# A Macaron block on one core: the first three down products made inside the last feature tile, loads written in program order, and split rooms that don't overlap

## The chip, the cores and the metric

The kernel runs on one core of a Trainium2 chip. Its time is the device time of one execution in microseconds (us); the kernel before takes 871.24 us (median of three runs, 870.94 to 872.25).

## The reference

One layer over 512 tokens of width 1,024, all in float32:

```python
x = x + 0.5 * swiglu_ffn(rmsnorm(x, g1), w_gate1, w_up1, w_down1)   # feature width 2816
x = x + hybrid_mixer(rmsnorm(x, gm), ...)                           # attention heads and trailing-mean pooling
x = x + 0.5 * swiglu_ffn(rmsnorm(x, g2), w_gate2, w_up2, w_down2)
x = rmsnorm(x, g3)

def swiglu_ffn(x, w_gate, w_up, w_down):
    return (silu(x @ w_gate) * (x @ w_up)) @ w_down
```

The change touches the two feed-forward stages. Tolerances are those of float32, so the kernel splits every operand of a matmul into a rounded high part and a low part (`fp32r`) and adds three products: high x high, high x low, low x high (`mm3`, L180).

## The kernel before

**Stages.** First feed-forward stage (0 to about 342 us), mixer (to about 530), second feed-forward stage (to the end). Each feed-forward stage has an upward part (`ffn_up`, L405), which goes through 22 tiles of 128 features (gate and up columns), and a downward part (class `Down`, L625).

**Upward part.** Tiles 0 to 4 are plain products. From tile 5 (`PLAIN`) on, a tile is one step of a loop (L569 to L612) in which the 2 x 2 blocks of weights and tokens are multiplied by seven products in place of eight (the Strassen-Winograd scheme): A11, S3, S2, A22, S1, A12, S4 in this order, each of 12 matmuls of 256 columns. S3 and A22 share a bank (`up_hi`); A11, S2, S1 share another (`acc`), and so does the last product, S4, which starts it anew after S1 has been copied out (L595, in `copy`, L559). Inside the loop the orders of PE, ACT and DVE are as written (`tc.manual_schedule`); `fetch(n + 2)` loads the raw weights of the tile after the next into one of two rooms of 2,048 columns (`down.pool`, tag `raw`), `sum13`/`sum24` make their block sums in two rooms of 1,024 (`wpool`, tag `raw`), and `high...`/`low...` split them into high parts (ACT) and low parts (DVE). In the last two tiles fetch(22) and fetch(23) find nothing to fetch.

**Downward part.** The 22 feature tiles pair up into 11 rows of blocks, and these into six groups g (five of two, one of one; `groups`, L622). Seven products again, each over the six groups: for each g `product(p6, g, S2, T2)`, `product(p1, g, A11, B11)`, `product(p5, g, S1, T1)`, then S3 x T3, S4 x B22, A12 x B21 and A22 x T4. The first name is a block of activations, the second one of weights. T1 to T4 are sums of weight blocks that GpSimd's DMAs make in DRAM during the upward part (`make_sums`, L671, `wsum`); B11 to B22 are read from `in_wB`. A call of `Down.product` (L744) takes `tokens` (split of the activations: ACT then DVE, and for S2 and A11 an update of the block, L730), `weights` (a load into a raw room, then a split: ACT casts, DVE subtracts), and then the matmuls: 12 of 512 columns per product of a full group. "T2 of pair 0" below is the weights of product T2 for g = 0, and so on; "product n" counts from 1.

**Rooms.** Raw weights go through a ring of rooms (`rooms`, `raw_tile`, L135). After the loop of tiles it is set anew (L619): two of `down.pool`, two of `wpool`, and in the second stage four of the residual pool behind them. Split weights go through a ring of four (`part_tiles`, L146): three rooms in one tile `parts_sb`, high parts from column 0 and low parts from column 3,136 on, 1,024 apart, and a fourth of two tiles of its own (`whi`, `wlo` in the profile). Parts of the loop of tiles start at column 16 (`SHIFT`) of their room and their low part another 32 further; parts of the down products start at column 0.

**Order.** Outside regions of `manual_schedule` the framework's scheduler orders each engine's instructions by program order, readiness and its own estimates, and may put instructions of the down products between those of the loop. The loads of `Down.weights`, of x and of xt go through `load_now` (L175): each alone in a manual region of SyncE (SP). An engine takes its instructions in order, and a DMA that must wait for its room keeps all that is behind it on SP waiting. The residual x is loaded again into its tiles during the first down part (eight loads of 256 KB, after g = 1 in the code); in the second, eight tiles xt and two gain rows (`gb`) are loaded at g = 2. `constants` (L222) loads small constants and, through DRAM, makes the extended bias table `ext_d`.

Of the kernel before, what the change touches and what calls it, by code (L numbers as in the profile page):

```python
# [8 lines left out]
F32 = mybir.dt.float32  # L9
# [7 lines left out]
P = 128  # L17
# [30 lines left out]
def layer(  # L48
# [93 lines left out]
    parts_sb = wpool.tile([P, 2 * (HILO * 1024 + 64)], F32R, tag="parts", name="parts", bufs=1)  # L142
# [3 lines left out]
    def part_tiles(at=0, apart=0):  # L146
# [27 lines left out]

    def load_now(dst, src):  # L175

        with tc.manual_schedule(engines={mybir.EngineType.SP}):
            nc.sync.dma_start(dst, src)
# [43 lines left out]
    def constants():  # L222
# [5 lines left out]

        flat = EXT - REL
        ext = temp()  # L230
        nc.sync.dma_start(ext[:NH, :REL], rel)
        far = temp()
        nc.vector.tensor_copy(far[:NH, :flat], ext[:NH, 0:1].to_broadcast([NH, flat]))
        nc.sync.dma_start(ext_d[:, flat:], ext[:NH, :REL])
        nc.sync.dma_start(ext_d[:, :flat], far[:NH, :flat])
# [169 lines left out]
    def ffn_up(norm, wA, down, loaded):  # L405
# [42 lines left out]
        todo.extend(norm.blocks(down.pool, aside))  # L448

# [117 lines left out]
        with tc.manual_schedule(engines={E.PE, E.DVE, E.Activation}):  # L567
            last_silu = last_place = last_sums = nothing
            for n in range(PLAIN, KF):  # L569
# [32 lines left out]
                nc.vector.tensor_tensor(u[:, :HT], up_lo, u[:, :HT], op=ALU.add)  # L602
                low24(n + 1)
                product(acc, cut(w22, 0, S), S4, False)
# [20 lines left out]
    class Down:  # L625
# [14 lines left out]
        def __init__(self, order, pair, block):  # L640
# [8 lines left out]

            self.steps = sorted(  # L650
# [48 lines left out]

        def weights(self, i, g):  # L700
# [3 lines left out]
            raw = raw_tile()[:, :n]  # L704
# [39 lines left out]
        def product(self, acc, g, a, i, further=False, scale=None):  # L744
# [4 lines left out]
            if self.n_sums < KF:  # L749
                self.make_sums(a[0][:, 0].bitcast(F32))  # L750
# [37 lines left out]
    with tc.tile_pool(name="act1", bufs=1, reuse_waits="tile") as apool:  # L788
# [4 lines left out]
        for g in range(G):  # L793
# [3 lines left out]
            if g == 1:  # L797

                x[:] = residual_tiles()
                for k in range(KD):  # L800
                    load_now(x[k], xT[k])
# [758 lines left out]
```

## Time and profile before

| | |
|---|---|
| median of three runs | 871.24 us (870.94 to 872.25) |
| the profiled execution | 870.76 us, its span 868.6 us |
| mean granted TensorE clock | 0.988 |
| busy: PE, weight loads (PEld), DVE, ACT, POOL | 841.5, 747.5, 710.1, 501.2, 124.3 us |
| DMA | 158.49 MB, 182 GB/s on average |
| tile loop, first stage | about 61 to 223 us |
| down products, first stage | about 231 to 342 us |
| down products, second stage | from 751 us on |

Busy times overlap. PE's matmuls follow each other without a gap where it isn't made to wait, so a window in which PE is busy all of the time and the granted clock is 1.00 is bound by PE. In rows of timelines the first number is the start, the second the duration, and brackets hold the idle time of the engine before the instruction with what ended it.

### The profile page before, as it was taken

What the parts mean: (1) busy time and instruction counts of PE and PEld (TensorE: products, weight loads), DVE (VectorE), ACT (ScalarE), POOL (GpSimd) and SP (SyncE); (2) the same over time, 40 slices, a digit from 0 to 9 for tenths busy, and PEclk for the clock granted to TensorE, in tenths of its full rate; (3) what the DMA queues carried; (4) which work ended last, traced back from release to release, by engine and by line L of the source; (5) the groups of instructions that cost most, each with busy time, mean ns of one, the idle gap of its engine ahead of it and who ended that gap; (6) DMA issues with size and microseconds to landing.
All of it is one profiled execution on the core that took longest, in us unless ns stands there. A gap on an engine that the chain in (4) does not pass through costs nothing.

```text
span 868.6 us, 14124 instructions
## 1 busy us (share of the span) xinstructions
PE 841.5 (97%) x5296; PEld 747.5 (86%) x5296; DVE 710.1 (82%) x1128; ACT 501.2 (58%) x852; POOL 124.3 (14%) x197
## 2 busy tenths in 40 slices
PE   9999999999799999989999999999999999899995
PEld 7889999999688887867877878889999999788885
DVE  7899999999588769686777576969989999777897
ACT  7455565566376546548747556436556556566572
POOL 0113222122300000120020000112222112300011
PEclk9999999999899999999999999999999999999998
DMA  8268979788996663322220136257979788997622
GB/s 290 55 189 222 254 221 242 224 209 196 296 274 199 208 197 114 107 85 86 73 73 25 49 97 231 84 146 211 241 237 236 209 216 213 294 348 248 209 95 97
DMA packets 71955, 158.49 MB, mean 182 GB/s; under 512 B 6080, under 2 KB 29136, under 8 KB 71504
## 3 DMA queue, kind: packets, MB, share of 16 engines
q1 hardware_dynamic: 49088, 111.45, 37.7%
q0 software_dynamic: 22656, 46.14, 24.9%
q8 instruction: 41, 0.67, 0.3%
q14 instruction: 26, 0.21, 0.1%
q10 hardware_dynamic: 144, 0.01, 0.0%
HBM read 153.38 MB, written 50.34 MB: 235 GB/s over the span
## 4 chain that ended last, share of the span: by engine, by line
PE 54%; DVE 4%; ACT 1%; issue 1%; DMA 1%; POOLq 0%; POOL 0%; ACTq 0%
PE mm L183 13%; PE mm L184 13%; PE mm L185 13%; PE a L183 4%; PE a L184 3%; PE a L185 3%; PE a L1175 1%; PE a L1121 1%; DMA raw<-in_wB_dram 1%; PE a L1163 1%; DVE t L1042 1%; PE a L1360 0%; PE a L1050 0%; ACT prob L1102 0%; DVE parts L124 0%
## 5 line engine op out<-in xcount | busy, mean ns | idle before, releaser
L123 ACT CAST parts<-raw 128x1024 fp32r<-128x1024 f32 (+2 forms) x81 | 78.3, 974 | 68.0 <-PE mm L184 19.1
L124 DVE TENSOR_TENSOR parts<-raw,parts 128x1024 fp32r<-128x1024 f32 (+2 forms) x81 | 90.7, 1128 | 21.4 <-ACT parts L123 20.6
L559 ACT ACTIVATE t<-mm 128x256 f32<-128x256 f32 x102 | 39.2, 385 | 109.2 <-PE mm L185 107.0
L680 POOL DMA_DIRECT2D wsum<-in_wB_dram x72 | 71.7, 1148 | 37.5 <-DMA wsum<-wsum 29.7
L183 PE MATMUL mm<-ha,parts 128*128 128x256 f32 x272 | 75.1, 276 | 0.0
L185 PE MATMUL mm<-ha,parts 128*128 128x256 f32 x272 | 75.1, 276 | 0.0
L184 PE MATMUL mm<-ha,parts 128*128 128x256 f32 x272 | 75.1, 276 | 0.0
L678 POOL COPY mark<-t 128x1 f32<-128x1 f32 x40 | 16.2, 404 | 396.8 <-DVE t L592 221.5
L183 PE MATMUL mm<-hhi,parts 128*128 128x512 f32 x160 | 63.3, 399 | 0.2 <-ACT parts L123 0.2
L470 DVE TENSOR_TENSOR parts<-raw,parts 128x512 fp32r<-128x512 f32 x68 | 62.4, 952 | 0.9 <-ACT parts L465 0.8
L185 PE MATMUL mm<-hhi,parts 128*128 128x512 f32 x160 | 62.4, 394 | 0.0
L184 PE MATMUL mm<-hlo,parts 128*128 128x512 f32 x160 | 62.1, 389 | 0.0
L124 DVE TENSOR_TENSOR ah<-acts,ah 128x512 fp32r<-128x512 f32 (+1 forms) x72 | 47.3, 666 | 16.6 <-ACT ah L123 14.4
L465 ACT CAST parts<-raw 128x512 fp32r<-128x512 f32 x68 | 56.4, 830 | 5.0 <-DMA raw<-in_wA_dram 2.5
L123 ACT CAST ah<-acts 128x512 fp32r<-128x512 f32 (+1 forms) x72 | 41.1, 581 | 27.1 <-PE mm L184 20.4
L184 PE MATMUL mm<-parts,ah 128*128 128x512 f32 x136 | 53.1, 391 | 0.0
L183 PE MATMUL mm<-parts,ah 128*128 128x512 f32 x136 | 53.0, 389 | 0.0
L185 PE MATMUL mm<-parts,ah 128*128 128x512 f32 x136 | 52.9, 389 | 0.0
L184 PEld LDWEIGHTS mm<-ha,parts 128*128 128x128 f32 x272 | 51.1, 188 | 0.1
L183 PEld LDWEIGHTS mm<-ha,parts 128*128 128x128 f32 x272 | 51.1, 188 | 0.1
L185 PEld LDWEIGHTS mm<-ha,parts 128*128 128x128 f32 x272 | 51.1, 188 | 0.0
L470 DVE TENSOR_TENSOR wlo<-wsum,whi 128x1024 fp32r<-128x1024 f32 x34 | 41.6, 1225 | 9.7 <-PE mm L185 7.2
(239 smaller groups left out, 2800.6 us busy)
## 6 DMA issues: line engine op xcount, KB each, us to landing
raw<-in_wA_dram SPq DMA_DIRECT2D x87, 512.0 KB, 6.1
wsum<-in_wB_dram POOLq DMA_DIRECT2D x60, 512.0 KB, 7.6
raw<-wsum SPq DMA_DIRECT2D x40, 512.0 KB, 4.6
raw<-in_wB_dram SPq DMA_DIRECT2D x30, 512.0 KB, 4.8
wsum<-wsum POOLq DMA_DIRECT2D x20, 512.0 KB, 5.1
x<-in_xT_dram SPq DMA_DIRECT2D x16, 256.0 KB, 7.3
raw<-in_wQK_dram SPq DMA_DIRECT2D x8, 512.0 KB, 3.5
raw<-in_wO_dram SPq DMA_DIRECT2D x8, 512.0 KB, 3.4
```

The costliest lines, as they stand in the source:

```text
L123: nc.scalar.copy(hi, src)
L124: nc.vector.tensor_tensor(lo, src, hi.bitcast(F32), op=ALU.subtract)
L183: nc.tensor.matmul(acc, a[0], b[0], start=start, stop=False, **more)
L184: nc.tensor.matmul(acc, a[0], b[1], start=False, stop=False, **more)
L185: nc.tensor.matmul(acc, a[1], b[0], start=False, stop=stop, **more)
L465: nc.scalar.copy(hi, src)
L470: nc.vector.tensor_tensor(lo, src, hi.bitcast(F32), op=ALU.subtract)
L559: nc.scalar.activation(dst, src, AF.Copy, scale=scale)
L678: nc.gpsimd.tensor_copy(mark, after[:, 0:1])
L680: nc.gpsimd.dma_start(self.rows(i, g), self.rows(self.terms[i][at], g), **(dict(accum_op=ALU.add) if at else {}),)
L1042: nc.vector.tensor_tensor(q3, q3, rs[:, t, :].unsqueeze(2).to_broadcast([P, 8, HD]), op=ALU.mult)
L1121: nc.tensor.matmul(sc[i][:, :n], qT[pair][0][a][rows, t * P : (t + 1) * P], kT[pair][0][b][rows, :n], start=a + b == 0, stop=a == 1,)
```

## The change

- **Loads.** From tile 2 on up to the end of the first stage, and in the second stage up to the first output, SP's instructions are issued in written order (`in_order`); `load_now` is gone. The loads of the first six weight tiles of the down products (T2, B11, T1 of pairs 0 and 1; `self.ahead`) are written into the last two tiles, in the places of the fetches that find nothing: T2 and B11 of pair 0 together in one room of 2,048 columns, T1 of pair 0 and T2 of pair 1 in the two rooms of the sums, B11 and T1 of pair 1 in the other room of 2,048.
- **First three products.** Their tokens and weights are split at written places inside the last tile (`first_tokens`, `first_weights`); `product` uses them and doesn't make them again.
- **Rings.** The order of the raw rooms after the loop changes (`more`, `own`, `own`, `more`; in the second stage the four rooms of the residual pool ahead of them).
- **Later loads.** x goes one load each behind the loads of products 8 to 15, constants behind 17, the bias table's load, fill and store behind 18, 20 and 25; in the second stage xt behind 8 to 15, the gain rows behind 16 and 17 (`self.then`).
- **Parts' rooms.** Each of the three rooms is 2,112 columns with the high part and the low part inside it, so that no room overlaps the next.

```diff
-    parts_sb = wpool.tile([P, 2 * (HILO * 1024 + 64)], F32R, tag="parts", name="parts", bufs=1)
+    parts_sb = wpool.tile([P, HILO * 2112], F32R, tag="parts", name="parts", bufs=1)
...
-            i = n_own[0] % HILO * 1024
+            i = n_own[0] % HILO * 2112
             n_own[0] += 1
-            hi, lo = (parts_sb[:, i + j * (HILO * 1024 + 64) :] for j in range(2))
+            hi, lo = parts_sb[:, i:], parts_sb[:, i + (1024 if apart else 1088) :]
         return hi[:, at : at + 1024], lo[:, at + apart : at + apart + 1024]
...
         todo.extend(norm.blocks(down.pool, aside))
+        in_order.enter_context(tc.manual_schedule(engines={mybir.EngineType.SP}))
...
                 w11, w13, w24 = (w[n, i][:2] for i in (11, 13, 24))
+                if n == KF - 1:
+                    down.load(new_sum())
+                    down.load(new_sum())
                 product(acc, w11, A11, True)
+                ends = n == KF - 1
...
                 product(up_hi, cut(w13, S, S), S3, True)
-                fetch(n + 2)
+                if n < KF - 2:
+                    fetch(n + 2)
+                else:
+                    down.load(down.pool.tile([P, 4 * S], F32, tag="raw", name=name("raw"), bufs=RAW))
                 high11(n + 1)
                 low11(n + 1)
+                if ends:
+                    down.first_tokens(0)
                 last_sums()
                 sum13(n + 1)
                 copy(z[:, HT:], up_hi, -1.0)
                 product(acc, cut(w24, 0, S), S2, False)
                 copy(u[:, HT:], acc, -1.0)
                 sum24(n + 1)
+                if ends:
+                    down.first_tokens(1)
                 product(up_hi, cut(w24, S, S), A22, False)
                 nc.vector.tensor_tensor(u[:, HT:], up_hi, u[:, HT:], op=ALU.add)
                 down.make_sums(u[:, HT:])
+                if ends:
+                    down.first_weights(0)
                 product(acc, cut(w13, 0, S), S1, False)
                 copy(z[:, :HT], acc)
...
                 high24(n + 1)
+                if ends:
+                    down.first_tokens(2)
                 product(up_lo, cut(w22, S, S), A12, True)
                 nc.scalar.activation(sg[:, HT:], z[:, HT:], AF.Silu)
                 nc.vector.tensor_tensor(u[:, :HT], up_lo, u[:, :HT], op=ALU.add)
                 low24(n + 1)
+                if ends:
+                    down.first_weights(1)
                 product(acc, cut(w22, 0, S), S4, False)
...
             last_silu()
             last_place()
+            down.first_weights(2)
             last_sums()
 
-        rooms[:] = [(down.pool, "raw", RAW, 4 * S)] * RAW + [(wpool, "raw", RAW, 1024)] * RAW
+        own, more = (wpool, "raw", RAW, 1024), (down.pool, "raw", RAW, 4 * S)
+        rooms[:] = [more, own, own, more]
         n_raw[0] = 0
...
+            self.ahead = [(i, g) for g in range(2) for i in (T2, B11, T1)]
+            self.loaded, self.then, self.made = {}, {}, []
...
+        def load(self, room):
+
+            if self.ahead:
+                i, g = self.ahead.pop(0)
+                raw = self.loaded[i, g] = room[:, :1024]
+                src = self.rows(i, g)
+                c = S if tuple(src.shape[1:]) == (groups[g][1], S) else groups[g][1] * P
+                nc.sync.dma_start(raw.rearrange("p (n c) -> p n c", c=c), src)
+                if room.shape[-1] > 1024:
+                    self.load(room[:, 1024:])
+
+        def first_tokens(self, n):
+            self.made.append([self.tokens((S2, A11, S1)[n], 0)])
+
+        def first_weights(self, n):
+            self.made[n].append(self.weights((T2, B11, T1)[n], 0))
+
         def weights(self, i, g):
...
-            raw = raw_tile()[:, :n]
+            raw = self.loaded.get((i, g))
+            new = raw is None
+            if new:
+                raw = raw_tile()[:, :n]
...
         def product(self, acc, g, a, i, further=False, scale=None):
-            a, w = self.tokens(a, g, scale), self.weights(i, g)
+            if self.n_products < len(self.made):
+                a, w = self.made[self.n_products]
+            else:
+                a, w = self.tokens(a, g, scale), self.weights(i, g)
             self.n_products += 1
...
+            for what, *args in self.then.get(self.n_products, ()):
+                what(*args)
             self.mms(acc, g, a, w, further=further)
...
-        ffn_up(n1, wA1, down1, loaded=False)
-        constants()
+        ffn_up(n1, wA1, down1, False, in_order)
+        x[:] = residual_tiles()
+        for k in range(KD):
+            down1.then[8 + k] = [(nc.sync.dma_start, x[k], xT[k])]
+        down1.then[17] = [(constants,)]
+        for k, what in zip((18, 20, 25), extended()):
+            down1.then[k] = [(what,)]
...
-        ffn_up(n3, wA2, down2, loaded=True)
-        xt = [hpool.tile([P, S], F32, tag="h", name=name("xt")) for _ in range(2 * NT)]
-        rooms.extend((xpool, f"x{i}", 1, 2 * S) for i in range(KD // 2))
-        gb = [temp(), temp()]
+        ffn_up(n3, wA2, down2, True, in_order)
+        xt, gb = [None] * (2 * NT), [None] * 2
+        rooms[:0] = [(xpool, f"x{i}", 1, 2 * S) for i in (3, 2, 1, 0)]
...
+        for i in range(2 * NT):
+            down2.then[8 + i] = [(again, i)]
+        for half in range(2):
+            down2.then[16 + half] = [(last_gain, half)]
...
         piece(len(todo))
+        in_order.close()
         for tt in range(2):
             residual(0, tt, p1[tt][0][0])
```

`again(i)` takes a tile xt and loads it, `last_gain` the same for a gain row; `extended` is the second half of `constants` in three steps.

More of the change, by code (lines that the diff above doesn't have):

```diff
@@ L173, in weights @@
         return hi, lo
-    def load_now(dst, src):
-        with tc.manual_schedule(engines={mybir.EngineType.SP}):
-            nc.sync.dma_start(dst, src)
     def mm3(acc, a, b, start, stop, further=False):
@@ L227, in constants, with extended, load, fill @@
             nc.gpsimd.memset(inv_count[:, t : t + 1], 1.0 / (t + 1))
+    def extended():
         flat = EXT - REL
[L230 to L235, printed above, removed]
+        ext, far = temp(), temp()
+        def load():
+            nc.sync.dma_start(ext[:NH, :REL], rel)
+        def fill():
+            nc.vector.tensor_copy(far[:NH, :flat], ext[:NH, 0:1].to_broadcast([NH, flat]))
+        def store():
+            nc.sync.dma_start(ext_d[:, flat:], ext[:NH, :REL])
+            nc.sync.dma_start(ext_d[:, :flat], far[:NH, :flat])
+        return load, fill, store
     def rsqrt_column(v):
@@ L402, in blocks, with ffn_up @@
             ]
-    def ffn_up(norm, wA, down, loaded):
+    def ffn_up(norm, wA, down, loaded, in_order):
         def evacuate(f, gate, up):
@@ L796, in layer @@
             down1.product(p5, g, S1, T1)
[L797 to L801, printed above, removed]
         p7 = whole(abank)
@@ L1351, in layer @@
             run_parts()
-    with tc.tile_pool(name="act2", bufs=1, reuse_waits="tile") as apool:
+    with tc.tile_pool(name="act2", bufs=1, reuse_waits="tile") as apool, ExitStack() as in_order:
         down2.begin(apool)
```

20 lines of the change are left out of this document (12 added, 8 removed).

## The prediction

> **What bounds the kernel now.** I read the page first, then the windows by stage, then the chain of waits of TensorE (PE), and around the two longest waits the timelines of PE, ScalarE (ACT), VectorE (DVE) and SyncE (SP). The page says PE:
>
> ```profile
> span 868.6 us, 14124 instructions
> ...
> PE 841.5 (97%) x5296; PEld 747.5 (86%) x5296; DVE 710.1 (82%) x1128; ACT 501.2 (58%) x852; POOL 124.3 (14%) x197
> ```
>
> PE is idle for only 868.6 - 841.5 = 27.1 us, so what can be won lies in its waits. The longest, from the view of waits (line, what ended the wait, us in total, times, longest):
>
> ```profile
> PE mm L183 <- ACT t L559: 5.5, 1, 5.5
> PE mm L183 <- ACT whi L123: 3.2, 1, 3.2
> ...
> PE a L183 <- ACT ah L126: 1.3, 1, 1.3
> ```
>
> The first two lie at the same place of the two feed-forward stages: where the last feature tile ends and the down products begin. PE's timeline there (start, duration):
>
> ```profile
> 222.65 0.28 PE L185 MATMUL mm<-ha,parts 128*128 128x256 f32 x1
> 228.40 0.58 PE L183 MATMUL mm<-sa,parts 128*128 128x256 f32 x1 [5.47 <-ACT t L559]
> ...
> 231.98 0.63 PE L183 MATMUL mm<-whi,ah 128*128 128x512 f32 x1
> 232.41 0.63 PE L184 MATMUL mm<-wlo,ah 128*128 128x512 f32 x1
> ...
> 237.93 0.39 PE L183 MATMUL mm<-parts,ah 128*128 128x512 f32 x1
> ...
> 747.24 0.28 PE L185 MATMUL mm<-sa,parts 128*128 128x256 f32 x1
> 750.76 0.50 PE L183 MATMUL mm<-whi,ah 128*128 128x512 f32 x1 [3.24 <-ACT whi L123]
> 752.02 0.73 PE L183 MATMUL a<-parts,ah 128*128 128x512 f32 x2 [0.75 <-ACT parts L123]
> ...
> 758.99 0.39 PE L183 MATMUL mm<-parts,ah 128*128 128x512 f32 x1
> ```
>
> The row at 237.93, and at 758.99 in the second stage, is the first matmul of the third down product (T1 of pair 0). The row at 231.98 starts 0.43 us before the next, where the steady rate is 0.227 (below): after the wait PE also runs at half rate for a while. The windows show that as the granted clock (columns: us, then busy us and count of PE, PEld, DVE, ACT, POOL, then PEclk, DMA share, GB/s):
>
> ```profile
> 195.55:205.07 9.52, 9.52 (x86) 9.52 (x85) 8.31 (x13) 5.57 (x11) 3.69 (x5) 1.00 0.99 216
> 205.07:214.60 9.53, 9.53 (x86) 9.53 (x85) 9.09 (x15) 5.60 (x11) 0.64 (x2) 1.00 0.67 162
> 214.60:222.77 8.17, 8.17 (x74) 8.13 (x72) 8.06 (x12) 5.72 (x11) 2.79 (x4) 1.00 0.94 247
> 222.77:237.93 15.16, 9.69 (x38) 8.24 (x37) 6.06 (x9) 4.41 (x7) 5.58 (x8) 0.77 1.14 309
> 237.93:248.81 10.88, 10.88 (x49) 9.01 (x48) 8.18 (x12) 5.23 (x7) 1.14 (x1) 1.00 1.14 293
> 747.36:758.99 11.63, 7.63 (x26) 5.74 (x25) 6.47 (x9) 5.44 (x8) 3.56 (x6) 0.85 1.07 330
> 250.00:260.00 10.00, 10.00 (x45) 7.90 (x44) 9.41 (x12) 9.97 (x16) 0.00 (x0) 1.00 0.89 262
> ```
>
> Why PE waits is read from ACT and SP:
>
> ```profile
> 227.02 1.04 ACT L123 CAST whi<-raw 128x1024 fp32r<-128x1024 f32 x1 [5.31 <-DMA raw<-in_wB_dram]
> 227.97 0.38 ACT L559 ACTIVATE t<-mm 128x256 f32<-128x256 f32 x1
> ...
> 749.67 1.04 ACT L123 CAST whi<-raw 128x1024 fp32r<-128x1024 f32 x1 [4.45 <-DMA raw<-in_wB_dram]
> ```
> ```profile
> 208.38 8.52 SPq L178 DMA_DIRECT2D raw<-wsum  x3
> ...
> 218.31 0.39 SPq L178 DMA_DIRECT2D raw<-in_wB_dram  x1
> 218.75 5.20 SPq L178 DMA_DIRECT2D x<-in_xT_dram  x6
> ...
> 741.13 1.08 SPq L178 DMA_DIRECT2D raw<-in_wB_dram  x2
> ```
>
> B11 of pair 0 is the second down product, but its load goes out only at 218.31, when its room (the last tile's raw weights) is free, with 1.5 MB of x loads right behind it, and lands at 227.0, 8.7 us later. ACT takes its instructions in order: the cast that waits for that load stands ahead of L559, which empties the bank that the tile's last product (S4) needs. So S4 waits too. In the second stage L559 stands ahead of the cast, S4 runs, and the wait is 3.2 us.
>
> **The two terms of the sum.** Between 222.77 and 237.93 PE has 12 matmuls of 256 columns (S4) and 24 of 512 (T2 and B11 of pair 0, 12 each). At the steady rates, 84 matmuls of 256 in the 9.53 us of one tile (0.1134) and 48 of 512 in 10.88 us (0.2267), that is 1.36 + 5.44 = 6.80 us. It took 15.16: 8.36 us lost, of which 5.6 is the wait and the rest the half rate. In the second stage the 24 took 11.63: 6.19 us lost. All that the change can win here is 14.55 us.
>
> **Part by part. (1) Loads.** T2 and B11 of pair 0 are asked for in the tile before the last, into one room of 2,048 columns, where fetch(22) used to find nothing to fetch: at 208.4, where T2's load stands today. The others go out as their rooms come free: T1 of pair 0 and T2 of pair 1 within the span of the first SP row, the last at about 216.6, B11 and T1 of pair 1 at 218.3. How long they take:
>
> ```profile
> DMA to landing us min/median/max: 4.4/9.0/10.1
> ```
>
> (the raw tiles' loads from 205 to 245). At the longest, B11 lands by 208.8 + 10.1 = 218.9, T1 of pair 0 by 216.6 + 10.1 = 226.7; then its cast (1.04) and low part (1.13) are done at 228.9.
>
> **(2) x and its like.** Eight x loads (in the second stage eight xt and two gain loads) leave the jam and go one per product behind products 8 to 17. From 250 to 260 a raw load of 512 KB per product of 2.72 us takes 262 GB/s in all with a DMA share of 0.89 (weight sums still running at its start). With 256 KB more per product it is 768 KB / 2.72 us = 289 GB/s, beside 309 and 330 GB/s in the rows of the jam. Cost taken: 0. Cover: four raw rooms, about three products (8 us) between a load and its use; without that cover, 8 x 256 KB at 300 GB/s, 7 us.
>
> **(3) Tokens and weights written into the last tile.** ACT and DVE get three token splits, three weight splits and two updates (L730) in a fixed order; most of it stood there already, put in by the scheduler (DVE 8.06 of 8.17 us from 214.60). DVE's prices are the distances of starts:
>
> ```profile
> 214.99 0.42 DVE L602 TENSOR_TENSOR t<-mm,t 128x256 f32<-128x256 f32 x1
> 215.33 1.22 DVE L470 TENSOR_TENSOR parts<-wsum,parts 128x1024 fp32r<-128x1024 f32 x1
> 216.46 0.68 DVE L690 TENSOR_TENSOR acts<-t,t 128x512 f32<-128x512 f32 x1
> 217.06 1.22 DVE L470 TENSOR_TENSOR parts<-raw,parts 128x1024 fp32r<-128x1024 f32 x1
> ```
>
> 0.34 for 256 columns, 0.60 for 512, 1.13 for 1,024. In the written order: from 218.2 two token splits and two updates to 220.6, the u sum to 220.9, T2's low part to 222.1; the z sum after S1 (PE ends it at 221.40, ACT copies until 222.0) to 222.4; the third tokens to 223.3; the u sum after A12 (222.77) to 223.6; B11's low part after ACT (whose cast can start at 223.0, after copy, tokens and Silu, and ends at 224.0) to 225.2; place to 225.8; T1's low part to 226.9, if its load is there as at the median. PE without a wait ends S4 at 222.77 + 1.36 = 224.13 and then needs T2 (ready 222.1), B11 at 226.85 (225.2) and T1 at 229.57 (226.9). Slack 2.0, 1.7 and 2.7 us: nothing on the path. If the scheduler slips tokens of pair 1 in between (1.2 us of DVE each with update), the 1.7 may shrink to nothing. Behind it a pair of three products needs 3 x 0.60 + 3 x 1.13 + 2 x 0.60 = 6.4 us of DVE in 8.16 of PE, so DVE gains on PE. Bounds of this part: 0 below (PE can't beat its rate), and one wait like the 0.75 or the 1.35 us of the rows above per stage. I take 0.4 per stage, 0.8 in all: with a slack of 1.7, nearer to nothing.
>
> **(4) Parts' rooms.** A part of the tile loop starts at column 16 of its room, one of the down products at 0, and rooms lie 1,024 apart: T2's room of pair 0 begins inside the last 16 columns of w22, which A12 reads until 222.77. T2's cast could not come before; with rooms of 2,112 it can after A11 (215.96). It is worth nothing alone, but part 3 needs it: otherwise T2's cast ends at 223.8 and its low part at about 225, 0.7 us after its second matmul wants it.
>
> **(5) SP in written order, the small loads.** SP waits at each load for its room with all later loads behind it. In the tile loop that is the order of fetches already. The bias table's store, at which SP stood until the table's load had landed, now comes seven products after that load:
>
> ```profile
> SPq L234 <- DMA t<-in_rel_dram: 6.2, 1, 6.2
> ```
>
>  The output queue is as before from the first output on. Own rooms and x rooms change places in the ring; both rings still hold four (eight) loads. I take 0.
>
> Sum against the profiled execution: its own time is 870.76 (span 868.6). 870.76 - 8.36 - 6.19 + 0.8 = 857.0. The median of the runs, 871.24, is 0.5 above that execution: 857.5.
>
> **Rivals.** (a) One stage keeps a wait: the scheduler puts a cast of a later weight, or a load comes late, ahead of what S4 or T2 needs. For it: that is what happened, and at only one of two equal places did it hold up S4. Against: all six first casts are now written in order, and the seventh (T2 of pair 1) needs a room that S4 frees. Price: up to all of a term: 857.5 + 6.2 = 863.7, or 857.5 + 8.4 = 865.9. Whether a wait of 2 or 3 us costs only itself hangs on the clock: after 5.47 us, and after 3.24 + 0.75 with one matmul between, PE ran at half rate, after the wait of 1.35 it did not. The Trainium skill, "TensorE: Matmul & The Clock Gate", Part 1, says the rate halves after an idle window of about 3.4 us and comes back after as long a busy one; the trace agrees, and by that rule a rest of 2 us would give 859.5 and not, with the 2.7 us of half rate of the first stage, 862.
>
> (b) The loads become the bound at products 8 to 17, as x and weights share a queue: 1 to 7 us, 858.5 to 864.5. For it: share 0.89 without x at 250 to 260. Against it: 289 GB/s are below what the jam moved, and loads run three products ahead. The Trainium skill, "DMA: Bandwidth & Descriptors", Specifications, puts HBM's limit per core at about 358 GB/s; by that limit 289 fit; the highest row here is 330.
>
> (c) The other side: hi and lo of a split now lie 1,088 columns apart and no longer 3,136; if the splits got slower by it, DVE would bound the tile loop. It is busy 8.31 and 9.09 of 9.5 us in two neighbouring tiles: 0.82 us of slack on average. To eat the whole gain (13.8 us over 34 tiles, 0.41 each) each tile's splits (3 x 1.13 + 0.60 = 4.0 us) must grow by 1.23 us, 31%; beyond that it is slower than before. At a third, 1.33 us, it is 34 x 0.51 = 17 us on 857.5: 875. Against it: the fourth room's hi and lo are tiles of 1,088 columns each, and cost the same:
>
> ```profile
> L470 DVE TENSOR_TENSOR wlo<-wsum,whi 128x1024 fp32r<-128x1024 f32 x12 | 14.7, 1226 | 4.3 <-PE mm L185 3.0 <-ACT whi L465 1.3
> L470 DVE TENSOR_TENSOR parts<-raw,parts 128x1024 fp32r<-128x1024 f32 x11 | 13.4, 1219 | 0.0
> ```
>
> (d) The change doesn't do what it says: the same work only waits elsewhere, as later loads start later, and time stays at 871. Against it: from 237.93 to 248.81 PE is busy all of the time with loads that were asked for in the jam, and DVE is busy 8.18 of 10.88 us.
>
> **How the numbers follow.** Forecast 0.66 (855.3 if the 1.35 us wait goes too, to 859); (a) 0.15; (b) 0.11; (c) 0.04; (d) 0.04. Range 855 to 864: it leaves out the upper end of (a) and (b), (c) and (d). 0.2% (1.7 us) is about what a measurement of this kernel can tell. Faster: forecast, (a) and (b), 0.92; same 0.04; slower 0.04.
>
> **What would show it.** Right: PE without a gap over 1 us and PEclk 1.00 from S4 to the third product in both stages; the first in_wB load of the down products issued at about 208.8 and 732; no ACT cast that waits for a DMA there; splits still 1.22 us. Wrong: a wait on a raw load in ACT between products 1 and 18, DVE at 10 of 10 in the tile loop, or a PE wait on `parts` at products 4 to 6.

## The result, and the profile after

The changed kernel takes 858.72 us (median of four runs, 857.39 to 859.28), the kernel before 871.75 us beside it: a ratio of 0.9847, 95% interval 0.9828 to 0.9865. In a later set (below) it took 857.17 us (five runs) against 873.44 (seventeen): 0.9818, 0.9795 to 0.9842. The forecast was 857.5. Two executions lie far outside all others, 1995.4 us with the old rooms and 2981.57 us of the kernel before beside another run, and no ratio below uses them. The profiled execution took 858.56 us, its span is 856.4, against 870.76 and 868.6 before: 12.2 us less. The page and PE's longest waits:

```profile
span 856.4 us, 14108 instructions
...
PE 838.5 (98%) x5296; PEld 745.4 (87%) x5296; DVE 709.1 (83%) x1128; ACT 501.0 (58%) x852; POOL 124.3 (15%) x197
```
```profile
PE a L1104 <- DVE t L1096: 1.4, 2, 1.1
...
PE mm L180 <- DVE m L1244: 1.0, 1, 1.0
...
PE mm L180 <- DVE parts L124: 0.4, 1, 0.4
```

The two waits that led the list before (5.5 and 3.2 us) are gone, and none has come to the top in their place. PE's timeline at the two handovers: first and last matmul of S4, first of T2 and of T1 of pair 0; then, in the second stage, first of T2 and of T1:

```profile
222.63 0.28 PE L179 MATMUL mm<-sa,parts 128*128 128x256 f32 x1
...
223.88 0.28 PE L181 MATMUL mm<-sa,parts 128*128 128x256 f32 x1
223.99 0.40 PE L179 MATMUL a<-parts,ah 128*128 128x512 f32 x1
...
229.46 0.39 PE L179 MATMUL mm<-parts,ah 128*128 128x512 f32 x1
...
741.35 0.40 PE L179 MATMUL a<-parts,ah 128*128 128x512 f32 x1
...
746.81 0.39 PE L179 MATMUL mm<-parts,ah 128*128 128x512 f32 x1
```

From S4's first matmul to T1's it is 229.46 - 222.63 = 6.83 us, where before it was 15.16; in the second stage, from T2's, 746.81 - 741.35 = 5.46, where it was 11.63. No row there has a bracket: PE has no gap. SP, ACT and DVE show why:

```profile
208.24 0.34 SPq L734 DMA_DIRECT2D raw<-wsum  x1
208.62 0.44 SPq L734 DMA_DIRECT2D raw<-in_wB_dram  x1
...
228.40 0.50 SPq L804 DMA_DIRECT2D x<-in_xT_dram  x1
```
```profile
223.12 1.04 ACT L123 CAST whi<-raw 128x1024 fp32r<-128x1024 f32 x1
...
249.59 1.05 ACT L123 CAST parts<-raw 128x1024 fp32r<-128x1024 f32 x1 [2.46 <-DMA raw<-in_wB_dram]
```
```profile
221.22 1.21 DVE L124 TENSOR_TENSOR parts<-raw,parts 128x1024 fp32r<-128x1024 f32 x1
224.94 1.22 DVE L124 TENSOR_TENSOR wlo<-raw,whi 128x1024 fp32r<-128x1024 f32 x1
226.68 2.35 DVE L124 TENSOR_TENSOR parts<-wsum,parts 128x1024 fp32r<-128x1024 f32 x2
```

B11's load goes out at 208.62 instead of 218.31, x's at 228.40 instead of 218.75. B11's cast at 223.12 waits for nothing. Further on ACT does wait for loads (2.56, 2.06, 1.83 and 2.46 us, the last in the row at 249.59), and PE feels one of these waits:

```profile
251.96 0.50 PE L180 MATMUL mm<-parts,ah 128*128 128x512 f32 x1 [0.35 <-DVE parts L124]
```

The windows (us, then busy us and count of PE, PEld, DVE, ACT, POOL, then PEclk, DMA share, GB/s) show a granted clock of 1.00 through both handovers, and 0.83 in two places of the mixer:

```profile
220.00:230.00 10.00, 10.00 (x64) 8.96 (x63) 9.96 (x16) 7.94 (x13) 5.80 (x8) 1.00 1.14 303
...
460.00:470.00 10.00, 9.20 (x49) 7.31 (x48) 7.71 (x31) 6.66 (x18) 0.00 (x0) 0.83 0.00 0
...
490.00:500.00 10.00, 8.38 (x31) 6.45 (x31) 5.77 (x8) 6.01 (x9) 0.00 (x0) 0.83 0.00 0
...
740.00:750.00 10.00, 10.00 (x53) 8.49 (x52) 9.96 (x15) 7.67 (x12) 4.58 (x7) 1.00 1.07 344
```

So the handovers gained 8.33 + 6.17 = 14.5 us, and the span 12.2. The experiments ask three things: which part of the change brings the gain, what the lost time was made of, and where the other 2.3 us are.

### The profile page after: what moved, and what is told of

Read it like the earlier page. It is cut to its first block, busy times and chain, and to the rows that moved or that the text cites. A ratio compares the mean times of both kernels' runs of the same rounds, so it can differ in the third digit from the quotient of the medians.

```text
span 856.4 us, 14108 instructions
## 1 busy us (share of the span) xinstructions
PE 838.5 (98%) x5296; PEld 745.4 (87%) x5296; DVE 709.1 (83%) x1128; ACT 501.0 (58%) x852; POOL 124.3 (15%) x197
## 4 chain that ended last, share of the span: by engine, by line
PE 56%; DVE 4%; ACT 1%; issue 1%; POOLq 0%; POOL 0%
PE mm L179 14%; PE mm L180 14%; PE mm L181 13%; PE a L179 4%; PE a L180 4%; PE a L181 4%; PE a L1229 1%; PE a L1175 1%; PE a L1217 1%; DVE t L1096 1%; PE a L1414 0%; PE a L1104 0%; ACT prob L1156 0%; DVE parts L124 0%; DVE o L1478 0%
## 5 line engine op out<-in xcount | busy, mean ns | idle before, releaser
L123 ACT CAST parts<-raw 128x1024 fp32r<-128x1024 f32 (+2 forms) x77 | 74.3, 971 | 66.5 <-PE mm L180 17.8
L124 DVE TENSOR_TENSOR parts<-raw,parts 128x1024 fp32r<-128x1024 f32 (+2 forms) x77 | 86.0, 1122 | 23.1 <-ACT parts L123 22.4
L123 ACT CAST ah<-acts 128x512 fp32r<-128x512 f32 (+1 forms) x72 | 40.6, 580 | 17.1 <-PE mm L180 13.6
L987 DVE TENSOR_TENSOR parts<-raw,parts 128x1024 fp32r<-128x1024 f32 x24 | 29.4, 1227 | 25.4 <-ACT parts L985 25.2
```

Source lines behind the costliest of these rows:

```text
L123: nc.scalar.copy(hi, src)
L124: nc.vector.tensor_tensor(lo, src, hi.bitcast(F32), op=ALU.subtract)
L987: nc.vector.tensor_tensor(lo, raws[i], hi.bitcast(F32), op=ALU.subtract)
```

## Experiments: which part brings the gain

**B11 of pair 0 late again.** The changed kernel, with B11 of pair 0 asked for where it was before:

```diff
-            self.ahead = [(i, g) for g in range(2) for i in (T2, B11, T1)]
+            self.ahead = [(T2, 0), (T1, 0), (T2, 1), (B11, 0), (T1, 1)]
```

B11 of pair 1 is no longer among the early loads either: its load goes out at 222.49, where the changed kernel has it at 218.05.

> The changed kernel with the load of B11 of pair 0 asked for where it was before the change, behind T1 of pair 0 and T2 of pair 1 (218.3 us in the first stage); the written order and the later x loads stay. Theory (the load is the cause, and with x out of the way it lands 5 to 9 us after it is asked for, at 223.3 to 227.3; PE needs it at 226.9): PE waits 0 to 2.5 us per stage, and not before S4 but before the product of B11; time 859 to 863. Rival (written order alone suffices): as the changed kernel, under 859.5. Rival (x has no part in the lateness): the load takes 8.7 us or more again and the time is 862 or above.

Measured: 865.15 us (862.88 to 867.91, five runs), ratio 0.9918 (0.9891 to 0.9945). ACT and PE at the handovers:

```profile
225.69 1.05 ACT L123 CAST whi<-raw 128x1024 fp32r<-128x1024 f32 x1 [2.43 <-DMA raw<-in_wB_dram]
```
```profile
228.05 0.50 PE L180 MATMUL mm<-wlo,ah 128*128 128x512 f32 x1 [0.76 <-DVE wlo L124]
...
750.28 0.50 PE L180 MATMUL mm<-wlo,ah 128*128 128x512 f32 x1 [0.76 <-DVE wlo L124]
```

B11 is asked for at 218.15 and lands 7.5 us later. With S4 no longer behind the cast, the late load costs 1.2 and 1.1 us at the handovers: the mechanism is the expected one, but the time is 2 us above the expected range. About 1 us more lies in the first down part. The rest is not a wait for the load: the upward part of the second stage takes 226.5 us up to S4 instead of 221.1. At its start PE's order is another one in this program (the first tile's products stand behind all transposes of x and not between them), and PE waits for 1.23 us, then

```profile
526.64 2.04 PE L338 MATMUL a<-t,ones 128*128 128x512 f32 x2 [2.05 <-DVE t L330]
```

with a granted clock of 0.83 in the window from 520 to 530. The mixer, on the other hand, took 2.6 us less than in the first profile of the changed kernel (table below). So of the 6.4 us between the two medians about 3 go with the late loads; the rest is the scheduler's order, less what the mixer gave back.

**The early load alone.** The kernel before, with T2 and B11 of pair 0 loaded into the empty room of the tile before the last, and nothing else changed:

```diff
+                if n == KF - 2:
+                    room = down.pool.tile([P, 4 * S], F32, tag="raw", name=name("raw"), bufs=RAW)
+                    for at, i in enumerate((T2, B11)):
+                        raw = down.loaded[i] = room[:, at * 1024 : at * 1024 + 1024]
...
+                        nc.sync.dma_start(raw.rearrange("p (n c) -> p n c", c=c), src)
```

> The kernel before with one edit: in the tile before the last, the fetch that found nothing to fetch asks for the weights of T2 and B11 of pair 0 into that room. The old rooms of parts, the scheduler's order of casts and all other loads stay, x's too. My theory: what cost the time was that one load, asked 10 us too late. Then B11's cast waits for no load, PE's waits of 5.5 and 3.2 us at the two handovers fall below 1 us each, and the time falls by 9 to 12 us, to 860 to 863 (what is missing to the changed kernel is T1's load in the jam of x's loads). The rival: the load is necessary but not enough, since the loads of x still go out ahead of the next ones and the third product or the next pair waits for its weights: then the waits only move to T1 and pair 1, each 2 to 5 us, and the time is 865 to 870.

Measured: 870.52 us (867.2 to 872.94, twelve runs) against 873.44, ratio 0.997 (0.9948 to 0.9992). The rival held in its mechanism; its time, 865 to 870, is just missed. The handovers are nearly as clean as in the changed kernel (7.09 us from S4 to T1 and 5.61 from T2 to T1, there 6.83 and 5.46), but the waits only moved. SP, DVE, ACT, PE and one window:

```profile
218.62 6.90 SPq L178 DMA_DIRECT2D x<-in_xT_dram  x7
228.28 0.35 SPq L178 DMA_DIRECT2D raw<-wsum  x1
...
748.85 0.32 SPq L178 DMA_DIRECT2D raw<-wsum  x1
```
```profile
238.03 0.21 DVE L233 COPY t<-t 8x127 f32<-8x127 f32 x1 [8.14 <-DMA t<-in_rel_dram]
```
```profile
239.79 1.05 ACT L123 CAST whi<-raw 128x1024 fp32r<-128x1024 f32 x1 [9.24 <-DMA raw<-wsum]
...
764.83 1.04 ACT L123 CAST whi<-raw 128x1024 fp32r<-128x1024 f32 x1 [11.74 <-DMA raw<-wsum]
```
```profile
239.43 0.79 PE L184 MATMUL mm<-parts,ah 128*128 128x512 f32 x1 [3.24 <-DVE parts L124]
...
765.93 0.79 PE L183 MATMUL mm<-whi,ah 128*128 128x512 f32 x1 [4.70 <-ACT whi L123]
```
```profile
755.00:765.00 10.00, 6.23 (x28) 4.83 (x26) 0.00 (x0) 0.17 (x1) 1.04 (x1) 0.98 1.00 261
```

In the first stage the next weights go out on SP behind the x loads, and the cast that waits for those of 228.28 (T1 of pair 1, in the fourth room, `whi`) takes the place of B11's. DVE also stands for 8.14 us at the copy for the bias table, whose 8 KB load is in the same jam (before it stood there for 3.18): the part of the change that looked smallest removes a wait that the larger part would have lengthened. In the second stage x has no part in it: the first load of xt goes out only at 767.65. The same weights, T1 of pair 1, are asked for at 748.85 and land 15.9 us later; the changed kernel asks for them at 735.55. So there it is the early load of these weights that is missing, not a later xt. From 755 to 765 DVE does nothing at all. After T1's first matmul the second stage takes 870.5 - 752.91 = 117.6 us, before 868.6 - 758.99 = 109.6: the 6.0 us won at its handover are all lost again, and 2.0 more.

**The early load, and the later loads moved in the code only.** The run above, with x, constants, bias table, xt and gain rows behind the products that the changed kernel names, but SP's order left to the scheduler:

```diff
+            for what, *args in self.then.get(self.n_products, ()):
+                what(*args)
             self.mms(acc, g, a, w, further=further)
...
+        for k in range(KD):
+            down1.then[8 + k] = [(load_now, x[k], xT[k])]
```

> The kernel before with the early load of T2 and B11 of pair 0 as in the run before this one, and with the later loads at the places of the changed kernel: x behind products 8 to 15, the constants behind 17, the bias table's load, fill and store behind 18, 20 and 25, in the second stage xt behind 8 to 15 and the gain rows behind 16 and 17. The splits stay in the scheduler's order, the rooms of parts as they were, and the loads of T1 of pair 0 and of pair 1 come where they came before. My theory: the early load clears the handover and the later ones keep it clear, and the two together are nearly all of the change: no PE wait over 1 us between the last tile and product 6 in either stage, no ACT wait of 5 us or more on the fourth weights, and 859 to 862 us. The rival: T1 of pair 0 and the loads of pair 1 have to be asked for early and in written order as well: then ACT still waits for one of them by 3 us or more, PE by 1.5 us or more in a stage, and the time is 863 to 868.

Measured: 870.62 us (866.61 to 872.66, twelve runs) against 871.95, ratio 0.9972 (0.9949 to 0.9995). SP and ACT:

```profile
217.13 0.33 SPq L178 DMA_DIRECT2D x<-in_xT_dram  x1
...
218.35 2.12 SPq L178 DMA_DIRECT2D x<-in_xT_dram  x4
```
```profile
237.98 1.04 ACT L123 CAST whi<-raw 128x1024 fp32r<-128x1024 f32 x1 [8.02 <-DMA raw<-wsum]
...
761.40 1.04 ACT L123 CAST whi<-raw 128x1024 fp32r<-128x1024 f32 x1 [11.21 <-DMA raw<-wsum]
```

My theory fell, and its test with it: x was not deferred, and the time lies above the rival's range too. A load's place in the code is not its place on SP; the scheduler sent x out from 217.13 on. So this run does not tell what late loads alone bring. It shows that `in_order`, the written order on SP, is what makes the later places real. No run has the early load of T2 and B11 and the written order without the four other early loads, so what those four are worth is not separated.

**x at once.** The changed kernel, with x loaded right behind the six early loads and the written order on SP kept:

```diff
-            down1.then[8 + k] = [(nc.sync.dma_start, x[k], xT[k])]
+            nc.sync.dma_start(x[k], xT[k])
```

> The changed kernel with the eight x loads of the first stage right behind the six early loads and not one per product. Theory: what PE needs at the handover is asked for before x, so nothing waits there; x and the loads of pair 2 then share the queue, and ACT's waits for loads move from products 8 to 12 to products 5 to 8, with at most 1 us of wait in PE: 858 to 860. Rival (the jam of x loads was itself the cause of the wait): a PE wait of several us at the handover, 862 or more.

Measured: 863.27 us (861.69 to 864.36, four runs), ratio 0.9896 (0.9863 to 0.9929). SP, ACT and PE:

```profile
219.13 9.54 SPq L847 DMA_DIRECT2D x<-in_xT_dram  x8
229.89 0.33 SPq L760 DMA_DIRECT2D raw<-wsum  x1
```
```profile
242.06 1.04 ACT L123 CAST parts<-raw 128x1024 fp32r<-128x1024 f32 x1 [10.77 <-DMA raw<-wsum]
```
```profile
243.16 0.49 PE L179 MATMUL a<-parts,ah 128*128 128x512 f32 x1 [2.59 <-ACT parts L123]
244.42 0.50 PE L180 MATMUL a<-parts,ah 128*128 128x512 f32 x1 [0.77 <-DVE parts L124]
```

Neither text held in full. The six early loads carry the handover (6.83 us from S4 to T1, as in the changed kernel), but the seventh waits on SP behind x, so the wait of several us comes one pair later, and the first down part takes 322.9 - 317.4 = 5.5 us longer. Deferring x is worth about 5 us in the first stage, once the early loads are there.

**Splits in the scheduler's order.** The changed kernel with all its loads, but `first_tokens` and `first_weights` empty.

> The changed kernel without the written tokens and weights in the last tile: the scheduler places the splits of the first three products, as before the change; the early loads stay. Theory (the late load of B11 was the cause, a cast ahead of the copy harms only while it waits): the B11 cast still stands ahead of the copy that frees S4's bank, but finds its data there; PE waits at most 0.5 us per stage, time 858.7 to 860. Rival (the order of ACT was the cause): the wait before S4 comes back in the first stage, 863 to 867.

Measured: 859.79 us (859.28 to 860.86, four runs), ratio 0.9859 (0.9832 to 0.9885). One wait of 0.67 us before S4 in the first stage, none in the second:

```profile
224.07 0.39 PE L179 MATMUL mm<-sa,parts 128*128 128x256 f32 x1 [0.67 <-ACT t L565]
```

Nearly as expected: with the loads right, no long wait comes back. By the profile the written splits bring 0.8 us at the first handover (7.62 us from the end of A12 to T1, where the changed kernel takes 6.83) and nothing at the second; the medians differ by 1.1 us, which is not clear of the spread.

**Old rooms.** The changed kernel with the rooms of `parts_sb` 1,024 apart, as before. In this kernel T2's cast overwrites the last 16 columns of w22 before A12 has read them, since the written order puts it ahead of A12: that part of the computation is changed.

> The changed kernel with the old, overlapping rooms for the split weights. Theory (the rooms matter because the written order needs them): the cast of T2 of pair 0 stands in ACT's order ahead of the copy that frees S4's bank, and now has to wait until A12 has ended, some 3 us later than with rooms of their own. S4 waits for that copy: PE idle for about 1.6 us before S4 in both stages, time 858.7 + 3 = 862, PE's clock stays at 1.00. Rival (the rooms do nothing, the loads are all): no wait before S4, 858.7.

Measured: 856.99, 859.71 and 855.89 us, ratio 0.9831 (0.9795 to 0.9867). The rival held: in the stretch from 215 to 225, at a granted clock of 1.00, T2's cast starts at 220.51 and A12 at 222.24, and no wait stands before S4. The rooms by themselves neither cost nor bring time that these runs can show.

## Experiments: what the lost time was made of

**PE kept busy.** The kernel before, with matmuls of a constant in PE's two long waits (their results are not used):

```diff
+                for _ in range(fill):
+                    nc.tensor.matmul(up_hi[:, :P], ones, ones, start=True, stop=True)
```

> The kernel before, with small matmuls that nobody reads put into PE's order at the two waits (22 before S4 in the first stage, 14 behind S4 in the second), so that PE isn't idle there. Theory (the half rate after the waits comes from the idle time before it, 2.7 us in the first stage and 1.8 in the second): the waits for the load stay, the granted clock stays at 1.00 and the time falls by up to 4.5 us, to about 867. Rival (the half rate has another cause, the DMA traffic for one): the clock falls again and the time stays at 871.

Measured: 872.1 us (868.76 to 874.33, ten runs) against 872.61, ratio 0.999 (0.9968 to 1.0012). A window, and PE:

```profile
222.00:232.00 10.00, 8.77 (x71) 8.18 (x70) 5.09 (x8) 4.84 (x9) 5.48 (x8) 1.00 1.15 321
```
```profile
231.32 0.50 PE L184 MATMUL a<-parts,ah 128*128 128x512 f32 x1 [0.81 <-DVE parts L124]
```

PEclk stays at 1.00, where it was 0.77 over 222.77 to 237.93: the half rate does come from the idle time. But nothing is won, since PE at full rate runs into splits that are late themselves. The way from A12's end to T1 gets 1.6 us shorter (13.6 for 15.16), and the first down part behind it 2.3 us longer (89.65 for 87.31), with new waits for splits of 0.76 and less around 250. The half rate lay beside work of ACT and DVE that the late load had pushed back; filling PE's idle time does not win it.

**x out of the way of B11.** The kernel before, with x's loads held back until the third pair of products is reached.

> The kernel before, with the x loads of the first stage held back until the tokens of pair 2's last product are there (a copy of one column on GpSimd into each x tile first). Theory (x loads right behind the load of B11 stretched its landing to 8.7 us): it lands after 4.4 to 6.5 us, PE's wait before S4 falls from 5.5 to 1 to 3 us, without the half rate the first stage gains 4 to 7 us, 864 to 867. Rival (the load is late because it is asked for late, and as long on its way without x): 870 to 871.

Measured: 870.22 us (867.96 to 873.85, ten runs), ratio 0.9973 (0.9953 to 0.9994). B11 is asked for at 217.62; ACT and PE:

```profile
225.93 1.04 ACT L123 CAST whi<-raw 128x1024 fp32r<-128x1024 f32 x1 [4.51 <-DMA raw<-in_wB_dram]
```
```profile
227.31 0.58 PE L183 MATMUL mm<-sa,parts 128*128 128x256 f32 x1 [4.66 <-ACT t L559]
```

Without x behind it B11 still takes 225.93 - 217.62 = 8.3 us, by this reckoning, where it took 8.7. The rival held: the load was asked too late, and x slowed it by little.

## Experiments: where 2.3 us stayed

**The mixer's last output projection.** The changed kernel, with the matmuls of one step reordered so that those of the low part of `m` come last. In the profile of the changed kernel PE waited there for 0.95 us, and the clock fell behind it.

```diff
+                if part and k == 3:
...
+                    for d in ab:
+                        nc.tensor.matmul(out_acc[d], ab[d][0], src[0], start=False, stop=False)
+                        nc.tensor.matmul(out_acc[d], ab[d][1], src[0], start=False, stop=False)
+                    for d in ab:
+                        nc.tensor.matmul(out_acc[d], ab[d][0], src[1], start=False, stop=True)
```

> The changed kernel, and in the mixer's output projection the last attention block's matmuls reordered: for each pair of output rows first the four matmuls that need only the block's high part, then the two that need its low part. Theory (the 1.6 us by which the changed kernel fell short of the sum lie in the mixer, where after two waits of 0.67 and 0.95 us PE's clock fell to half for 3.5 us, which it did not in the kernel before): the wait of 0.95 us goes, the clock stays at 1.00 there, 858.7 - 0.9 - 1.5 = 856.3, and the runs differ by less among themselves. Rival (the shortfall is elsewhere, or the clock falls anyway): 857.8 to 858.7.

Measured: 855.79 us (853.8 to 856.48, four runs) against 872.61, ratio 0.9821 (0.9789 to 0.9852). The wait shrank (the row below), PEclk was 1.00 throughout the mixer, and the mixer took 198.2 us instead of 201.6.

```profile
490.81 0.74 PE L1341 MATMUL mm<-m,parts 128*128 128x512 f32 x2 [0.24 <-DVE m L1244]
```

**x's loads later still.** The changed kernel, with x behind products 21 to 29 (`for k, at in enumerate((21, 22, 23, 24, 26, 27, 28, 29))`).

> The changed kernel with the x loads of the first stage behind products 21 to 29 and not 8 to 15. Theory (the loads and the weight sums together make ACT wait for loads at products 6 to 12, which PE feels once, 0.35 us): ACT no longer waits for a load between products 6 and 12, PE's wait of 0.35 us goes, 858.2. Rival (ACT's waits there come from the rooms, not from the transfers): ACT's waits stay and so does the time.

Measured: 857.72 us (857.06 to 858.1, four runs), ratio 0.9839 (0.9813 to 0.9866). PE's wait of 0.35 is gone, and the first down part (T1's first matmul to the mixer's first transpose) takes 317.02 - 229.97 = 87.05 us instead of 317.37 - 229.46 = 87.91. That this is the work of the later x is not shown. The reordered kernel and the one with scheduled splits have x behind 8 to 15 and take 87.05 and 87.04 us, without such a wait. And ACT still waits for loads, for 1.32 us at 240.48 and 1.17 at 246.63, which the theory had ruled out. The mixer's clock fell to 0.83 here too.

**Both, beside the changed kernel itself.** Measured side by side, five runs each.

> The changed kernel with both later edits: x's loads behind products 21 to 29 instead of 8 to 17, and the last output projection of the mixer in the order that lets the low parts come later. My theory: the two places are independent, so their gains add: PE's waits of 0.35 us (first down part) and 0.95 us (mixer) are both gone or below 0.3, PEclk is 1.00 in all windows of the mixer, and the time is 855 to 856, about 3 us below the changed kernel on the same chip. The rival: the time is set by the chip's clock and not by these waits; then the sum of the two edits is no better than the better one of them alone, and within 1.7 us of the changed kernel.

> The changed kernel, unedited, on the same chip as the two others of this set, for comparison. Both theories: 857.4 to 859.3 us as before. If the theory on the mixer holds, its profile shows PEclk below 1.00 near 490 to 500 us where the time is 858 or more, and 1.00 where it is 857.4 or less.

Measured: both edits 856.67 us (856.24 to 857.82), the changed kernel 857.17 (855.61 to 858.0), against 873.44. The rival held: 0.5 us, within the spread. (In the profile with both edits the mixer and the first down part are short, but the upward part of the second stage has waits of 0.56 and 1.01 us that the first profile of the changed kernel has not.) The unedited kernel's mixer ran without any drop of the clock this time. Its windows and its row of the wait; and the same wait in the first profile of the changed kernel, with a later matmul of each:

```profile
460.00:470.00 10.00, 8.80 (x51) 6.53 (x51) 7.81 (x31) 6.27 (x16) 0.00 (x0) 1.00 0.01 2
...
490.00:500.00 10.00, 8.38 (x38) 6.59 (x37) 6.26 (x8) 6.44 (x10) 0.00 (x0) 1.00 0.00 0
```
```profile
492.62 0.50 PE L180 MATMUL mm<-m,parts 128*128 128x512 f32 x1 [0.95 <-DVE m L1244]
...
494.13 0.39 PE L180 MATMUL mm<-m,parts 128*128 128x512 f32 x1
```
```profile
492.90 0.50 PE L180 MATMUL mm<-m,parts 128*128 128x512 f32 x1 [0.95 <-DVE m L1244]
...
494.01 0.63 PE L180 MATMUL mm<-m,parts 128*128 128x512 f32 x1
```

The same kernel, the same wait: once half rate follows (0.63), once full rate (0.39). Set by the stretches of half rate in the 10 us windows from 450 to 510, the mixer's length in all profiles but that with the old rooms (first transpose ahead of it to first transpose behind it) is as follows. A stretch that crosses the edge of two windows counts once: 0.92 and 0.91 with the early load alone, 0.93 and 0.90 with the later loads in the code.

| stretches below 1.00 | mixer, us |
|---|---|
| none | changed kernel again 199.0; late B11 198.9; reordered 198.2 |
| one | before 199.9; scheduled splits 200.0; x at once 199.8; x later (kernel before) 200.0; filled 200.5; x at 21 to 29 200.5; both edits 199.4 |
| two | changed kernel, first profile 201.6; early load alone 201.6; later loads in the code 201.5 |

One stretch of half rate costs about 0.8 to 1.6 us, and whether it comes differs between executions of one kernel. The two reordered kernels are the shortest of their rows, by 0.7 and 0.5 us (198.90 - 198.21, 199.84 - 199.36); the wait shrank by 0.95 - 0.24 = 0.71. So the reading that the reordered kernel seemed to confirm, 1.5 us of the shortfall made by this wait, is wrong: of the 3.3 us less in its mixer, most was the clock of that execution. No run here shows a kernel that is faster than the changed one by more than the spread.

## Why the prediction was right, point by point

- **The two terms.** Sized at 8.36 and 6.19 us; the handovers gave 15.16 - 6.83 = 8.33 and 11.63 - 5.46 = 6.17. The reading of PE's, ACT's and SP's rows (a late load, ACT in order, S4's bank not emptied) was the cause: B11 late again brings the wait for its load back, and x out of its way does not remove it. The half rate belongs to these terms only together with the wait, as the filled wait shows.
- **Step 1, loads.** B11 was asked for at 208.62 (worked out: 208.8), and all six casts found their data. In the second stage its load went out at 725.98 and not at 732: that figure fits the times of the kernel before (741.13 less one tile of 9.5) and leaves out that the stage now runs 6 us earlier (T2 at 741.35, before at 747.36).
- **Step 2, x.** Cost taken as 0, with four raw rooms, about 8 us, as the cover. The cover was too short by the prediction's own row (9.0 us to landing in the middle); in the changed kernel the raw loads from 225 to 252 take 8.5 to 13.0 us, and ACT waits for four of them by 1.8 to 2.6 us. The prediction named just that, a wait of ACT on a raw load between products 1 and 18, as a sign of being wrong. The sign was badly chosen: the kernel before has such waits too (2.68 us at 245.28), and PE feels only one of the four, by 0.35 us. That the cost was nearly 0 is thus in part luck. The stretch from T1's first matmul to the mixer takes 87.9 us against 325.2 - 237.93 = 87.3: 0.6 us, which the reordered kernel and the scheduled splits, with the same x loads, do not have. What this step gains was undervalued: it appears in the prediction only as a move out of the jam, and it is worth about 5 us, without which the early loads don't pay in full. In the sum that was hidden, because the terms were taken as won in full.
- **Step 3, order.** Low parts of T2 and B11 were ready at 222.4 and 226.2 (worked out 222.1 and 225.2). T1's, worked out as 226.9, is one of the row of two from 226.68 to 229.03, since the scheduler put a split of pair 1 beside it, as feared. PE needed T1's at about 229.7. The slack shrank, to 0.7 if T1's is the second of the two; PE waited for nothing, and the 0.8 taken for both stages was 0.05.
- **Step 4, rooms.** The conclusion "worth nothing alone" holds; the mechanism does not. With overlapping rooms and the written order the cast doesn't wait for A12, it runs where it is written, ahead of A12, and no 0.7 us are lost: what is lost is w22's last columns. The separate rooms permit the order and are no term of time.
- **Step 5, the table.** Taken as 0 and 0 in the changed kernel; but with the early load alone DVE's stall at this table grew from 3.18 to 8.14 us.
- **The shortfall.** The sum gave 857.0 for the profiled execution, measured 858.56. By the profile: 0.05 instead of 0.8 at the handovers, but 0.6 for loads in the first down part (0.1 was won ahead of it), 1.6 in the mixer and 0.2 in the second stage's upward part. The 1.6 is the clock of that execution: the other profiled one had the mixer at 199.0 and took 857.17. So the median's distance to the forecast, 1.2 us in one set and 0.3 in the other, says little; what was forecast is borne out by the two terms.
- **Rivals.** (a) and (d) did not come here, but they describe the early load alone, where the waits moved to pair 1. (b) did not come at products 8 to 17 but for the 0.35 us; a jam of that kind, at product 7, is what x at once shows, and that its 863.27 lies in the 858.5 to 864.5 worked out for other products is chance. That the trace agrees with the rule on the clock under (a) holds for the waits that are named there, not for the whole trace: the kernel before fell to 0.83 from 470 to 480 too, behind waits of 0.42, 0.23 and 0.15 us. (c) is out; the splits cost what they did:

```profile
L476 DVE TENSOR_TENSOR parts<-raw,parts 128x1024 fp32r<-128x1024 f32 x34 | 41.4, 1218 | 0.0
```

## What to carry to other kernels

A load that arrives late under an in-order engine is mended by asking for it earlier only if what then goes out behind it is put in order too: the early load alone won 3 us, where the changed kernel won 16 in the same set, because the loads next in line became the next late ones. Look at what stands behind the stalled instruction on every queue, the 8 KB loads included, and check in the trace that a moved load really goes out where the code has it. And before a difference of 1 or 2 us in one profile is explained, take a second profile of the same kernel.

## What was not expected of the hardware

- PE's clock fell to half behind waits of 0.67 and 0.95 us with one matmul's 0.5 us between them (matmuls 0.43 us apart from 493.59 to 496.57, about 3.3 us), in one execution and not in another of the same kernel with the same two waits. The Trainium skill, "TensorE: Matmul & The Clock Gate", Part 1, gives, in its table of the two states, an idle window of about 3.4 us as the cause and says that this window runs freely; the length of the slow stretch and the difference between executions agree with that, the idle time, 1.62 us in all, does not.
- After a wait of 2.59 and one of 0.77 us (x at once) PE also fell to half: matmuls 0.43 us apart from 245.62 on. Behind the single wait of 0.67 us with the splits in the scheduler's order, the window from 220 to 230 shows 1.00.
- A load of 512 KB took 8.3 us with x out of the way, at a DMA share of 1.08 (217.60 to 226.00 in that run) with GpSimd's weight sums going on; in the second stage of the early load alone, with no x or xt load about, one took 15.9 us, and its cast waited for 11.74.
